# The end of a decoder layer: rows normed and stored before the last expert column, whose tokens' rows are then made per slot and scattered

## The chip, the core and the metric

One core of a Trainium2 chip runs one program that holds a whole decoder layer. The core has TensorE (PE in the profile, its weight loads PEld), VectorE (DVE), ScalarE (ACT), GpSimd (POOL) and SyncE (SP), which here issues nearly all DMAs. The metric is the device time of one execution in microseconds (us). Three runs of the kernel before took 1240.55, 1242.22 and 1242.86 us, so the median is 1242.22 us.

## The reference, cut to what matters

The layer takes 512 tokens of 1024 features through a token mixer, a cross-attention and a mixture of 64 experts, each followed by a residual sum and a layer norm. The change touches the end alone: the last experts, their sum into the rows, and the third norm.

```python
def hierarchical_moe(x, ...):      # each token picks one group, then two experts in it
    ...
    hb = jax.nn.silu(xb @ w_gate[e]) * (xb @ w_up[e])     # D_EXPERT = 256
    return hb @ w_down[e]
    ...
    y_rows = y_rows * row_w[:, None]
    y = jax.ops.segment_sum(y_rows, row_tok, num_segments=N)   # added into the tokens' rows

h = layer_norm(ALPHA * h + ff, ln3_g, ln3_b)    # (r - mean) * rsqrt(var + eps) * g + b, per row of 1024
```

## The kernel before, in words

All expert weights, 192 MB in 64 experts of three matrices of 1 MB, are streamed from HBM once. The experts are served in 21 columns of 128 slots: a column holds one expert with 128 slots, two with 64 or four with 32 (`COLS`). A slot holds one token's row, or none. For each column PE multiplies the gathered rows with the gate and the up matrices (`hidden`, L1190: for a column of four, 64 matmuls each), ACT and DVE make silu(gate) times up (L1195, L1196), PE turns it, DVE copies the turned tile (`hT`), and PE multiplies with the down matrices. `split` (L255 on ACT, L256 on DVE) scales the result by the slot's routing weight and splits it into a high part `yh` and a low part `yl`, which fp32r matmuls can take. `combine` (L1415) then multiplies two columns' `yh` and `yl` with one-hot matrices (slot to token) and DVE adds the eight 128x512 results to `acc` (L1416), the residual rows of all 512 tokens as four tiles `t` of 128 rows, in two halves `nh`. `acc` is named `h` in the trace.

The weights go through ten slots of 1 MB. SP issues a weight's DMA once PE has finished with the slot's former content, so the order of the DMAs is fixed and SP waits in it. The down matrices of the last column come in three pieces of columns (`LASTD`: 512, 256, 256; L184). Every DMA of SP stands in one queue, in the order in which the program issues it.

The last column, number 20, holds four experts with 32 slots each. In the kernel before it ends like this. After the gate matmuls, PE copies halves of `acc` into PSUM by a matmul with the identity (L1484), for tiles 0 to 2; later the column's own one-hot matmuls (L1525) add its part there. Tile 3 is added by DVE (L1535). So no row of any token is complete before the last down matrices are used. Only then come the statistics of all four tiles (L1529, L1531), the inverse root on POOL (L97), and the norm of 512 rows of 1024: on ACT, DVE and POOL for five half tiles (L1574, L1578, L1579), on DVE alone for three (L1585, L1586). Each half tile is stored by its own DMA of 256 KB (L1590). The gain `g3` and the bias `b3` are loaded to all 128 partitions by two DMAs of 512 KB, behind the last weights in SP's queue (L1505, L1506). A loop over overflow slots follows (L1613); in these runs it has no turn.

The order on PE and POOL, and on SP, is made by a scheduler; a `manual_schedule` block keeps DVE (and ACT, where named) in program order.

Of the kernel before, what the change touches and what calls it, by code (L numbers as in the profile page):

```python
# [61 lines left out]
def tile_layer(ctx, tc, x, mem, positions, w_in, attn_sinks, conv_w, conv_b, b_igate, b_fgate, ml_norm_g,  # L62
# [20 lines left out]
    def row(ap1d):  # L83
        return ap1d.rearrange("(o n) -> o n", o=1)
# [14 lines left out]
    class LayerNorm:  # L99
# [7 lines left out]
        def stats(self, c):  # L107
            V.bn_stats(self.st[:, c, :], self.r[:, c * 512:(c + 1) * 512])
# [1363 lines left out]
    zs = {}  # L1472

    def half(nh):
        return slice(nh * 512, (nh + 1) * 512)

    def rows_in(halves):
        if not psl:
            pb.close()
            psl.append(ctx.enter_context(tc.tile_pool(name="psL", bufs=6, space=PSUM, reuse_waits="tile")))  # L1480
        psL = psl[0]
        for nh, t in halves:
            zs[t, nh] = psL.tile([P, 512], F32, name=f"pc_l{t}{nh}", tag="psL")
            T.matmul(zs[t, nh], lhsT=ident, rhs=acc[:, t, half(nh)], start=True, stop=False)  # L1484

    psl = []
# [14 lines left out]
    out_tiles()
    yh = strm.tile([P, 1056], F32R, name="yh_l", tag="wh", bufs=2)[:, :D]
    yl = strm.tile([P, 1056], F32R, name="yl_l", tag="wl", bufs=2)[:, :D]
    g3, b3 = [strm.tile([P, 1056], F32, name=n_, tag="wr", bufs=4)[:, :D] for n_ in ("g3", "b3")]
    nc.sync.dma_start(g3, row(ln3_g).to_broadcast([P, D]))  # L1505
    nc.sync.dma_start(b3, row(ln3_b).to_broadcast([P, D]))  # L1506
    oh = strm.tile([P, 1056], F32R, name="oh_l", tag="wr", bufs=4)[:, :S]
    V.tensor_scalar(oh, iota_f, tokf[:, c:c + 1], None, op0=ALU.is_equal)
    ph = psH.tile([P, 512], F32, name="ph_l", tag="psH")[:, :2 * P].rearrange("p (k n) -> p k n", k=2)
    for k in range(2):  # L1510
        T.transpose(ph[:, k, :], hb[:, k, :], ident)
    hT = hTs[c % 2]
    V.tensor_copy(hT, ph)
    ctx.enter_context(tc.manual_schedule(engines={mybir.EngineType.DVE}))

    def down_part(pd, o, n):
        for k in range(2):
            for sl, w in parts_of(c):
                T.matmul(pd[sl, :], lhsT=hT[:, k, sl], rhs=w['d'][:, k, o:o + n], start=(k == 0), stop=(k == 1))
        split(yh[:, o:o + n], yl[:, o:o + n], pd, wtab[:, c:c + 1])  # L1520

    def combine_part(z, o, n, ts, first, last):
        for y in (yh, yl):
            for t in ts:
                T.matmul(z[t][:, o % 512:o % 512 + n], lhsT=oh[:, t * P:(t + 1) * P], rhs=y[:, o:o + n],  # L1525
                         start=first and y is yh, stop=last and y is yl)
# [6 lines left out]
    def add_last(nh, z):  # L1533
        zs[3, nh] = outt[3][:, half(nh)]
        V.tensor_tensor(zs[3, nh], acc[:, 3, half(nh)], z, ALU.add)  # L1535
# [10 lines left out]
    rows_in([(1, 0), (1, 1), (1, 2)])  # L1546
    (o0, n0), (o1, n1), (o2, n2) = LASTD
    z0, z1 = [{t: zs[t, nh] for t in range(3)} for nh in range(2)]
    pd0 = psH.tile([P, 512], F32, name="pd_l0", tag="psH")
    down_part(pd0, o0, n0)  # L1550
    pd1 = psU.tile([P, 512], F32, name="pd_l1", tag="psU")
    down_part(pd1[:, :n1], o1, n1)
    combine_part(z0, o0, n0, range(3), False, True)
    z0[3] = psH.tile([P, 512], F32, name="pc_l30", tag="psH")
    combine_part(z0, o0, n0, [3], True, True)
    for t in range(3):
        stats(t, 0)
# [12 lines left out]
    stats(2, 1)  # L1570
    shift2(0)

    def norm3(t, nh):
        A.activation(outt[t][:, half(nh)], zs[t, nh], AF.Identity, bias=nb3[:, t:t + 1], scale=rs3[:, t:t + 1])  # L1574

# [3 lines left out]
        G.tensor_tensor(o, o, b3[:, half(nh)], ALU.add)  # L1579
        store(t, nh)  # L1580

    def all3(t, nh):

        o = outt[t][:, half(nh)]
        V.scalar_tensor_tensor(o, zs[t, nh], mv3[:, t, 0:1], g3[:, half(nh)], op0=ALU.subtract, op1=ALU.mult)  # L1585
        V.scalar_tensor_tensor(o, o, rs3[:, t:t + 1], b3[:, half(nh)], op0=ALU.mult, op1=ALU.add)  # L1586
        store(t, nh)

    def store(t, nh):
        nc.sync.dma_start(out[t * P:(t + 1) * P, half(nh)], outt[t][:, half(nh)])  # L1590

    for t, nh in ((0, 0), (0, 1), (1, 0)):
        norm3(t, nh)

    stats(3, 1)
    rsqrt2(2)
    gain3(0, 0)
    shift2(2)
    norm3(2, 0)
    norm3(3, 0)  # L1600
    gain3(0, 1)
    gain3(1, 0)
    all3(1, 1)
    gain3(2, 0)
    gain3(3, 0)
    all3(2, 1)
    all3(3, 1)


    psL = (psl[0], "psL")  # L1610
# [77 lines left out]
```

## Time and profile before

| | |
|---|---|
| median of three runs | 1242.22 us |
| the profiled execution's own time | 1243.13 us |
| its span, first to last instruction | 1241.3 us |
| PE busy | 1145.4 us, 92% |
| DVE busy | 614.3 us, 49% |
| ACT busy | 368.9 us, 30% |
| POOL busy | 123.7 us, 10% |
| mean granted TensorE clock | 0.972 of full speed |

The shares are means over the whole layer and say little about its end. The page's chain of waits is empty for this kernel, so the end is read from the timeline, where each row gives the start, the duration, the engine, the line and tile, and in brackets how long the engine was idle and what released it.

### The profile page before, as it was taken

The numbers are of one execution on the slowest core, as the hardware profiler recorded it, in microseconds if no ns is written. First come the engines' busy times: TensorE is split into PE (matmuls) and PEld (weight loads), VectorE is DVE, ScalarE is ACT, GpSimd is POOL, SyncE is SP. The second block draws the span as 40 slices with busy tenths as digits, with TensorE's granted clock in tenths as the row PEclk, the third lists the DMA queues.
The fourth block names the chain that finished last, engine by engine and source line by source line (L and its number), as shares of the span: only waits on it lengthen the run. The fifth ranks groups of instructions, "written<-read, shape, count | busy, mean of one in ns | idle before, by whom it ended". The sixth has DMA issues, their size and how long they took to land.

```text
span 1241.3 us, 18439 instructions
## 1 busy us (share of the span) xinstructions
PE 1145.4 (92%) x7201; PEld 841.6 (68%) x7201; DVE 614.3 (49%) x1407; ACT 368.9 (30%) x705; POOL 123.7 (10%) x118
## 2 busy tenths in 40 slices
PE   7999999999999999999999989899979998988982
PEld 6777777777787888788888876565735564654641
DVE  5668986533325434584354677834314342431326
ACT  4334355444425423254434341111101011111101
POOL 1330010000010101142101120000000000000003
PEclk8999999999999999999999989999989899998997
DMA  7221112222223233735306059999999999999993
GB/s 189 84 70 51 52 51 68 60 77 68 69 84 85 85 100 99 237 102 169 103 18 234 5 237 374 400 418 419 411 419 417 406 407 418 395 419 419 418 404 128
DMA packets 119658, 269.09 MB, mean 217 GB/s; under 512 B 18704, under 2 KB 79120, under 8 KB 95504
## 3 DMA queue, kind: packets, MB, share of 16 engines
q1 hardware_dynamic: 119280, 266.83, 57.4%
q8 instruction: 58, 0.95, 0.3%
q10 hardware_dynamic: 288, 1.05, 0.3%
q14 instruction: 32, 0.26, 0.1%
HBM read 265.76 MB, written 2.10 MB: 216 GB/s over the span
## 4 chain that ended last, share of the span: by engine, by line


## 5 line engine op out<-in xcount | busy, mean ns | idle before, releaser
L239 ACT CAST wh<-wr 128x1024 fp32r<-128x1024 f32 (+1 forms) x106 | 111.1, 1050 | 257.3 <-issue 82.0
L240 DVE TENSOR_TENSOR wl<-wr,wh 128x1024 fp32r<-128x1024 f32 (+1 forms) x80 | 99.5, 1245 | 152.1 <-ACT wh L239 149.1
L1190 PE MATMUL pu<-wu,arenaL 128*32 128x256 f32 (+2 forms) x1024 | 103.1, 441 | 30.4 <-DMA wu<-in_w_up_dram 30.3
L240 POOL TENSOR_TENSOR wl<-wr,wh 128x1024 fp32r<-128x1024 f32 x26 | 64.7, 2489 | 443.6 <-ACT wh L239 406.7
L1190 PEld LDWEIGHTS pu<-wu,arenaL 128*32 128x32 f32 (+2 forms) x1024 | 53.9, 134 | 75.3 <-DMA wu<-in_w_up_dram 41.2
L1196 DVE TENSOR_TENSOR arenaR<-arenaR,pu 128x256 f32<-128x256 f32 x21 | 13.1, 622 | 175.5 <-ACT arenaR L1195 175.5
L1190 PE MATMUL pu<-wg,arenaL 128*32 128x256 f32 (+2 forms) x1024 | 83.7, 390 | 6.4 <-DMA wg<-in_w_gate_dram 6.4
L1247 PE MATMUL px<-G,h2h 128*128 128x256 f32 (+1 forms) x320 | 81.1, 292 | 0.0
L1271 PE MATMUL pd<-wd,arenaR 128*32 128x512 f32 (+2 forms) x480 | 77.2, 596 | 3.0 <-DMA wd<-in_w_down_dram 2.8
L1190 PEld LDWEIGHTS pu<-wg,arenaL 128*32 128x32 f32 (+2 forms) x1024 | 46.7, 121 | 46.7 <-issue 10.5
L1248 PE MATMUL px<-G,h2l 128*128 128x256 f32 (+1 forms) x320 | 77.6, 282 | 0.0
L1195 ACT ACTIVATE arenaR<-pu 128x256 f32<-128x256 f32 x21 | 8.1, 386 | 211.2 <-PE pu L1190 211.2
L1247 PEld LDWEIGHTS px<-G,h2h 128*128 128x128 f32 x320 | 60.9, 190 | 7.3 <-issue 7.3
L255 ACT ACTIVATE yh<-pd,wtab 128x512 fp32r<-128x512 f32 x40 | 27.2, 687 | 124.9 <-PE pd L1271 110.7
L1415 PE MATMUL pc<-yh,oh 128*128 128x512 f32 x144 | 59.7, 415 | 1.9 <-DVE h L1416 1.8
L1248 PEld LDWEIGHTS px<-G,h2l 128*128 128x128 f32 x320 | 61.1, 191 | 0.1
L1416 DVE TENSOR_TENSOR h<-h,pc 128x512 f32<-128x512 f32 x72 | 49.3, 686 | 17.5 <-PE pc L1415 16.6
L1415 PE MATMUL pc<-yl,oh 128*128 128x512 f32 x144 | 56.8, 395 | 0.0
L1271 PEld LDWEIGHTS pd<-wd,arenaR 128*32 128x32 f32 (+2 forms) x480 | 22.4, 118 | 44.6 <-issue 35.5
L97 POOL TENSOR_TENSOR rs<-ve,pow_h 128x2 f32<-128x2 f32 x2 | 1.9, 956 | 496.5 <-DVE ve L1539 496.5
L1170 ACT ACTIVATE arenaL<-px,gbk 128x256 f32<-128x256 f32 (+1 forms) x44 | 24.2, 555 | 79.1 <-PE px L1248 70.1
L256 DVE SCALAR_TENSOR_TENSOR yl<-pd,wtab,yh 128x512 fp32r<-128x512 f32 x40 | 29.7, 749 | 32.3 <-ACT yh L255 32.0
(451 smaller groups left out, 2655.5 us busy)
## 6 DMA issues: line engine op xcount, KB each, us to landing
wg<-in_w_gate_dram SPq DMA_DIRECT2D x64, 1024.0 KB, 12.5
wu<-in_w_up_dram SPq DMA_DIRECT2D x64, 1024.0 KB, 14.6
wd<-in_w_down_dram SPq DMA_DIRECT2D x60, 1024.0 KB, 13.2
wr<-in_w_in_dram SPq DMA_DIRECT2D x50, 512.0 KB, 3.6
wr<-in_w_xkv_dram SPq DMA_DIRECT2D x16, 512.0 KB, 4.0
wr<-in_w_att_branch_dram SPq DMA_DIRECT2D x8, 512.0 KB, 4.0
wr<-in_w_ml_branch_dram SPq DMA_DIRECT2D x8, 512.0 KB, 4.0
wr<-in_w_mix_out_dram SPq DMA_DIRECT2D x8, 512.0 KB, 3.9
```

Source lines behind the costliest of these rows:

```text
L239: A.copy(hi, raw)
L240: (G if i % 4 == 3 else V).tensor_tensor(lo, raw, hi.bitcast(F32), ALU.subtract)
L255: A.activation(hi, src, AF.Copy, scale=scale)
L256: V.scalar_tensor_tensor(lo, src, scale, hi.bitcast(F32), op0=ALU.mult, op1=ALU.subtract)
L1170: A.activation(XT[:, k, :n], px[:, j, :n], AF.Identity, scale=gbk[:, 0, k:k + 1], bias=gbk[:, 1, k:k + 1])
L1190: T.matmul(pu[sl, u * 256:(u + 1) * 256], lhsT=XT[:, k, o + sl.start:o + sl.stop], rhs=w[what][:, k, :], start=(k == 0), stop=(k == NK - 1))
L1196: V.tensor_tensor(hb.rearrange("s k p -> s p k"), hs.rearrange("s (p k) -> s p k", k=2), pu[:, 256:512].rearrange("s (p k) -> s p k", k=2) ...
L1247: T.matmul(px[:, j, :n], lhsT=h2hv[:, t, 2 * c + j, :], rhs=g[:, t, :n], start=(t == 0), stop=False)
L1248: T.matmul(px[:, j, :n], lhsT=h2lv[:, t, 2 * c + j, :], rhs=g[:, t, :n], start=False, stop=(t == NT - 1))
L1271: T.matmul(pd[sl, :], lhsT=hT[:, k, sl], rhs=w['d'][:, k, nh * 512:(nh + 1) * 512], start=(k == 0), stop=(k == 1))
L1415: T.matmul(pc, lhsT=oh[:, t * P:(t + 1) * P], rhs=y[:, ns], start=(i == 0), stop=(i == len(mms) - 1))
L1416: V.tensor_tensor(acc[:, t, ns], acc[:, t, ns], pc, ALU.add)
```

## The change

Before the last column's matmuls, the change treats `acc` as if the last column did not exist: all 512 rows get their statistics, norm, gain and bias (`rows_meanwhile`, hooked in behind the gate matmuls) and are stored by four DMAs of 512 KB. DVE's part of the statistics is placed by hand between the adds of `combine`. Tokens that have a slot in the last column are stored with a wrong row by this. Their right rows are made a second time, one row per slot: `gsel` picks the row of each slot's token out of `acc` by fp32 matmuls (`slot_rows`, into `zf`), and `same`, a 128x128 matrix that says which slots have the same token, adds `yh` and `yl`. One tile of 128 rows is then normed on DVE into `fin`, and an indirect DMA of POOL scatters its rows to `out` by the tokens' numbers `tok_u`; empty slots have number 4096 and are left out. The scatter waits for all four stores, since it writes over some of their rows.

The gain and bias rows come as two DMAs of 2x512 in ACT's queue, long before, and are spread to 128 partitions by four matmuls with K=4 (`spread_row`) and four copies on ACT. The identity matmuls into PSUM, the 12 pairs of one-hot matmuls of the last column (L1525) and the two 512 KB loads go. The one-hot `oh` stays for the overflow loop, but is made last. The read of the loop's count (`nov_r`, one TENSOR_LOAD on each engine) moves ahead of the last column.

```diff
     c = NMAIN - 1
...
+    rows4 = work.tile([4, 512], name="rows4", at=0)
+    for i, v in enumerate((ln3_g, ln3_b)):
+        nc.scalar.dma_start(rows4[2 * i:2 * i + 2, :], v.rearrange("(a n) -> a n", a=2))
...
+    V.tensor_scalar(diag, ident, tokl, None, op0=ALU.mult)
+    T.matmul(prow, lhsT=ones, rhs=diag, start=True, stop=True)
+    V.tensor_scalar(same, prow, tokl, None, op0=ALU.is_equal)
+    for t in range(NT):
+        V.tensor_scalar(gsel[:, t, :], prow, -BIGIDX, rowid[:, t:t + 1], op0=ALU.add, op1=ALU.is_equal)
...
     run(combine(before, "last"))
-    hooks = {(0, 7): lambda: rows_in([(0, 0), (0, 1), (0, 2)])}
-    hb = hidden_of(c, (psU, "psU"), hooks)
+    ctx.enter_context(tc.manual_schedule(engines={mybir.EngineType.DVE, mybir.EngineType.Activation}))
     nov_r = nc.values_load(ovi[0:1, 32:33], min_val=0, max_val=NOV)
...
+    def spread_row(i):
+        pg = psL.tile([P, 512], F32, name=f"pg{i}", tag="psL")
+        T.matmul(pg, lhsT=ident[:4, i:i + 1].to_broadcast([4, P]), rhs=rows4, start=True, stop=True)
+        A.copy((g3, b3)[i // 2][:, half(i % 2)], pg)
+    def slot_rows(i):
+        o, w_ = LASTD[i]
+        zf.append(psL.tile([P, 512], F32, name=f"zf{i}", tag="psL")[:, :w_])
+        for t in range(NT):
+            T.matmul(zf[i], lhsT=gsel[:, t, :], rhs=acc[:, t, o:o + w_], start=(t == 0), stop=False)
+    def rows_meanwhile():
...
+        wstream.ahead(used[0] + COLS[c][0] + len(wslots))
+        out_tiles()
+        for i in (0, 1):
+            spread_row(i)
+        for t in range(2):
+            for nh in range(2):
+                stats(t, nh)
+        rsqrt2(0)
...
+        gain_row(0)
+        shift2(2)
+        norm_row(2)
+        norm_row(3)
+        bias_row(0, G)
+        gain_row(1)
+        bias_row(1, G)
+        gain_row(2)
+        slot_rows(0)
+    hb = hidden_of(c, (psU, "psU"), {(0, 7): rows_meanwhile})
+    slot_rows(1)
     for k in range(2):
         T.transpose(ph[:, k, :], hb[:, k, :], ident)
+    slot_rows(2)
     hT = hTs[c % 2]
+    gain_row(3)
     V.tensor_copy(hT, ph)
+    bias_row(2, V)
+    for i, (o, w_) in enumerate(LASTD):
...
+        split(yh[:, o:o + w_], yl[:, o:o + w_], pd, wtab[:, c:c + 1])
+        if i == 1:
+            bias_row(3, V)
+    for i, (o, w_) in enumerate(LASTD):
         for y in (yh, yl):
+            T.matmul(zf[i], lhsT=same, rhs=y[:, o:o + w_], start=False, stop=(y is yl))
+        for j in range(0, w_, 256):
+            V.bn_stats(stf[:, (o + j) // 256, :], zf[i][:, j:j + 256])
+    V.bn_aggr(mvf, stf)
+    V.tensor_scalar(vef, mvf[:, 1:2], LN_EPS / ALPHA ** 2, None, op0=ALU.add)
+    rsqrt_cols(rsf, vef, 1)
+    for z, (o, w_) in zip(zf, LASTD):
+        V.scalar_tensor_tensor(fin[:, o:o + w_], z, mvf[:, 0:1], g3[:, o:o + w_], op0=ALU.subtract, op1=ALU.mult)
+    for nh in range(2):
+        V.scalar_tensor_tensor(fin[:, half(nh)], fin[:, half(nh)], rsf, b3[:, half(nh)], op0=ALU.mult, op1=ALU.add)
+    G.indirect_dma_start(out, bass.IndirectOffsetOnAxis(ap=tok_u, axis=0), fin, None, bounds_check=S - 1, oob_is_err=False)
+    V.tensor_scalar(oh, iota_f, tokl, None, op0=ALU.is_equal)
```

Here `stats` is a BN_STATS of one half tile of `acc` (L1504) and, after the second half, a BN_AGGR (L1506); `norm_row`, `gain_row` and `bias_row` each treat 128 rows of 1024 on ACT, DVE, and POOL or DVE; `bias_row` also issues the store.

Two places show the new order. The first is DVE around the last `combine`, from the `yl` parts of column 19 (`yl_10119`) to the adds to `acc` (`h_3991`; `pc_last` are the results of `combine`). Before:

```order
L256 SCALAR_TENSOR_TENSOR yl_10119<-pd_10121,wtab,yh_10118 128x512
L256 SCALAR_TENSOR_TENSOR yl_10119<-pd_10132,wtab,yh_10118 128x512
L1416 TENSOR_TENSOR h_3991<-h_3991,pc_last_10152 128x512
L1416 TENSOR_TENSOR h_3991<-h_3991,pc_last_10158 128x512
L1416 TENSOR_TENSOR h_3991<-h_3991,pc_last_10164 128x512
```

And now (`oh_l` holds `same`, `arenaL` holds `gsel`, `st` and `mv` the statistics):

```order
L256 SCALAR_TENSOR_TENSOR yl_10119<-pd_10121,wtab,yh_10118 128x512
L1490 TENSOR_SCALAR oh_l<-prow,tokf 128x128
L1492 TENSOR_SCALAR arenaL<-prow,arenaR 128x128
L256 SCALAR_TENSOR_TENSOR yl_10119<-pd_10132,wtab,yh_10118 128x512
L1492 TENSOR_SCALAR arenaL<-prow,arenaR 128x128 x3
L1416 TENSOR_TENSOR h_3991<-h_3991,pc_last_10171 128x512
L1416 TENSOR_TENSOR h_3991<-h_3991,pc_last_10177 128x512
L1499 TENSOR_LOAD ovi
L1504 BN_STATS st_10147<-h_3991 128x6
L1416 TENSOR_TENSOR h_3991<-h_3991,pc_last_10183 128x512
L1504 BN_STATS st_10147<-h_3991 128x6
L1416 TENSOR_TENSOR h_3991<-h_3991,pc_last_10189 128x512
```

Five selection matrices now stand ahead of the first add, and a load, four statistics and an aggregation between the first add and the last. PE's last `combine` matmuls wait for these adds, since `pc_last` has two PSUM tiles.

The second place is PE in the last column, from the last gate matmul (`wg`) to the first up matmul (`wu`). Before:

```order
L1190 MATMUL pu_10200<-wg_10060,arenaL 32x256
L1484 MATMUL pc_l_10239<-h_3991,ident 128x512
L1484 MATMUL pc_l_10241<-h_3991,ident 128x512
L1484 MATMUL pc_l_10243<-h_3991,ident 128x512
L1190 MATMUL pu_10200<-wu_10072,arenaL 32x256
```

And now (`pg` are the spread gain and bias, `zf` the slots' rows):

```order
L1190 MATMUL pu_10241<-wg_10060,arenaL 32x256
L1549 MATMUL pg_10292<-arenaR,ident 128x512
L1549 MATMUL pg_10295<-arenaR,ident 128x512
L1549 MATMUL pg_10312<-arenaR,ident 128x512
L1549 MATMUL pg_10315<-arenaR,ident 128x512
L1557 MATMUL zf_10333<-h_3991,arenaL 128x512 x4
L1190 MATMUL pu_10241<-wu_10072,arenaL 32x256
```

Eight fp32 matmuls of 512 columns stand where three stood.

## Rows read from the trace of the kernel before

**Rows 1.** Windows of two stages: us, busy us by engine (instructions), TensorE clock, DMA.

```profile
1194.90:1206.80 11.90, 10.63 (x135) 5.12 (x134) 0.69 (x1) 0.02 (x1) 0.00 (x0) 1.00 1.02 401
1220.50:1236.20 15.70, 0.00 (x0) 0.00 (x0) 14.68 (x25) 3.60 (x5) 9.72 (x7) 0.62 0.27 99
```

**Rows 2.** Timeline, PE in the last column: start, us, line, shapes, [idle before].

```profile
1194.89 3.66 PE L1190 MATMUL pu<-wg,arenaL 128*32 128x256 f32 x64
...
1198.49 2.84 PE L1484 MATMUL pc_l<-h,ident 128*128 128x512 f32 x6
...
1203.11 3.64 PE L1190 MATMUL pu<-wu,arenaL 128*32 128x256 f32 x58 [1.21 <-DMA wu<-in_w_up_dram]
...
1207.86 0.44 PE L1511 MATMUL ph_l<-ident,arenaR 128*128 128x128 f32 x2 [1.11 <-DVE arenaR L1196]
...
1210.80 2.79 PE L1519 MATMUL pd_l<-wd,arenaR 128*32 128x512 f32 x32
...
1217.20 1.07 PE L1519 MATMUL pd_l<-wd,arenaR 128*32 128x256 f32 x16
```

**Rows 3.** Timeline, DVE around the last combine.

```profile
1187.50 0.75 DVE L256 SCALAR_TENSOR_TENSOR yl<-pd,wtab,yh 128x512 fp32r<-128x512 f32 x1 [0.96 <-ACT yh L255]
...
1188.16 1.36 DVE L1416 TENSOR_TENSOR h<-h,pc_last 128x512 f32<-128x512 f32 x2
...
1195.00 0.69 DVE L1416 TENSOR_TENSOR h<-h,pc_last 128x512 f32<-128x512 f32 x1 [0.23 <-PE pc_last L1415]
```

**Rows 4.** Groups by form, 1180 to 1242 us: count, busy us, mean ns, idle before.

```profile
L1416 DVE TENSOR_TENSOR h<-h,pc_last 128x512 f32<-128x512 f32 x8 | 5.5, 687 | 2.0 <-PE pc_last L1415 2.0
...
L1168 DVE TENSOR_SCALAR arenaL<-px,gbk 128x128 f32<-128x128 f32 x1 | 0.4, 411 | 1.5 <-ACT arenaL L1170 1.5
```

**Rows 5.** The line that loads the loop's count: duration in ns (min/median/max), start.

```profile
L1491 PEldq TENSOR_LOAD <-ovi x1: 488/488/488, 1204.9 to 1204.9; - x1
...
L1491 DVEq TENSOR_LOAD <-ovi x1: 812/812/812, 1235.4 to 1235.4; - x1
```

**Rows 6.** Timeline, the last column's split, statistics and last result.

```profile
1212.79 0.69 ACT L255 ACTIVATE yh_l<-pd_l,wtab 128x512 fp32r<-128x512 f32 x1 [5.62 <-PE pd_l L1519]
...
1218.85 0.48 DVE L256 SCALAR_TENSOR_TENSOR yl_l<-pd_l,wtab,yh_l 128x256 fp32r<-128x256 f32 x1
...
1219.26 0.68 DVE L1529 BATCH_NORM_STATS2 st<-out 128x6 f32<-128x512 f32 x1
...
1220.57 0.21 DVE L1531 BATCH_NORM_AGGREGATE mv<-st 128x2 f32<-128x12 f32 x1
...
1224.38 1.21 POOL L97 TENSOR_TENSOR rs<-ve,pow_h 128x2 f32<-128x2 f32 x1 [1.81 <-DVE ve L1539]
...
1235.36 0.75 DVE L1586 SCALAR_TENSOR_TENSOR out<-out,rs,b 128x512 f32<-128x512 f32 x1
```

**Rows 7.** Operations on 128x1024, whole trace: groups by form, and one line (ns).

```profile
L1081 ACT ACTIVATE h<-h,ln_nb,ln_rs 128x1024 f32<-128x1024 f32 x4 | 5.0, 1246 | 2.7 <-DVE ln_nb L119 2.7
...
L240 POOL TENSOR_TENSOR wl<-wr,wh 128x1024 fp32r<-128x1024 f32 x26 | 64.7, 2489 | 443.6 <-ACT wh L239 406.7 <-DVE pT L592 36.9
...
L1097 DVE TENSOR_TENSOR h<-h,bbc x4: 1224/1225/1226, 784.0 to 795.9; 128x1024 f32<-128x1024 f32 x4
```

**Rows 8.** One line of DVE at the end: from PSUM, and from SBUF beside POOL.

```profile
L1585 DVE SCALAR_TENSOR_TENSOR out<-pc_l,mv,g x2: 735/736/736, 1228.0 to 1231.9; 128x512 f32<-128x512 f32 x2
L1585 DVE SCALAR_TENSOR_TENSOR out<-out,mv,g x1: 1743/1743/1743, 1233.6 to 1233.6; 128x512 f32<-128x512 f32 x1
```

**Rows 9.** DMA issues: count, KB each, us from issue to landing.

```profile
out_dram<-out SPq DMA_DIRECT2D x1, 256.0 KB, 2.6
...
gbc<-in_ln_g_dram SPq DMA_DIRECT2D x1, 512.0 KB, 3.4
...
bif<-in_b_igate_dram SPq DMA_DIRECT2D x1, 2.0 KB, 7.1
```

**Rows 10.** A window in which PE waited for weights, columns as in rows 1.

```profile
1124.00:1128.00 4.00, 1.47 (x10) 0.38 (x14) 0.00 (x0) 0.00 (x0) 0.00 (x0) 0.64 1.02 424
```

More of the change, by code (lines that the diff above doesn't have):

```diff
@@ L1471, in tile_layer @@
     ve3, rs3, nb3 = [small.tile([P, NT], F32, name=n) for n in ("ve3", "rs3", "nb3")]
-    zs = {}
+    stf, mvf = small.tile([P, 4, 6], F32, name="stf"), small.tile([P, 2], F32, name="mvf")
+    vef, rsf = [small.tile([P, 1], F32, name=n) for n in ("vef", "rsf")]
+    tok_u = small.tile([P, 1], U32, name="tok_u")
+    xt1 = XTs[1].rearrange("p k n -> p (k n)")
+    gsel = xt1[:, 0:S].rearrange("p (t n) -> p t n", t=NT)
+    diag, fin = xt1[:, S:S + P], xt1[:, 1024:2048]
+    rows4 = work.tile([4, 512], name="rows4", at=0)
@@ new lines, in tile_layer @@
+    for i, v in enumerate((ln3_g, ln3_b)):
+        nc.scalar.dma_start(rows4[2 * i:2 * i + 2, :], v.rearrange("(a n) -> a n", a=2))
+    oh = strm.tile([P, 1056], F32R, name="oh_l", tag="wr", bufs=4)
+    oh, same = oh[:, :S], oh[:, S:S + P]
+    g3, b3 = [strm.tile([P, 1056], F32, name=n_, tag="wr", bufs=4)[:, :D] for n_ in ("g3", "b3")]
+    tokl = tokf[:, c:c + 1]
+    V.tensor_copy(tok_u, tokl)
+    V.tensor_scalar(diag, ident, tokl, None, op0=ALU.mult)
+    prow = psX.tile([P, 512], F32, name="prow", tag="psX")[:, :P]
@@ L1474, in half @@
+    T.matmul(prow, lhsT=ones, rhs=diag, start=True, stop=True)
+    V.tensor_scalar(same, prow, tokl, None, op0=ALU.is_equal)
+    for t in range(NT):
+        V.tensor_scalar(gsel[:, t, :], prow, -BIGIDX, rowid[:, t:t + 1], op0=ALU.add, op1=ALU.is_equal)
     def half(nh):
         return slice(nh * 512, (nh + 1) * 512)
[L1477 to L1484, printed above, removed]
@@ L1501, in tile_layer @@
[L1501 to L1508, printed above, removed]
@@ L1509, in tile_layer @@
[L1509 to L1526, printed above, removed]
+    zs = {}
     def stats(t, nh):
@@ L1580, in gain3 @@
         store(t, nh)
[L1582 to L1587, printed above, removed]
     def store(t, nh):
         nc.sync.dma_start(out[t * P:(t + 1) * P, half(nh)], outt[t][:, half(nh)])
[L1592 to L1610, printed above, removed]
+    def out_tiles():
+        for i in range(2):
+            pool, tag = wslots[wstream.next % wstream.total]
+            wstream.next += 1
+            t = pool.tile([P, 2048], F32, name=f"out{i}", tag=tag)
+            outt.extend([t[:, 0:D], t[:, D:2 * D]])
+    def norm_row(t):
+        A.activation(outt[t], acc[:, t, :], AF.Identity, bias=nb3[:, t:t + 1], scale=rs3[:, t:t + 1])
@@ new lines, in gain_row, with bias_row @@
+    def gain_row(t):
+        V.tensor_tensor(outt[t], outt[t], g3, ALU.mult)
+    def bias_row(t, on):
+        on.tensor_tensor(outt[t], outt[t], b3, ALU.add)
+        nc.sync.dma_start(out[t * P:(t + 1) * P, :], outt[t])
+    def spread_row(i):
[7 more added lines that the diff above has]
+            T.matmul(zf[i], lhsT=gsel[:, t, :], rhs=acc[:, t, o:o + w_], start=(t == 0), stop=False)
@@ new lines, in tile_layer @@
+    pb.close()
+    psL = ctx.enter_context(tc.tile_pool(name="psL", bufs=6, space=PSUM, reuse_waits="tile"))
+    zf = []
+    def rows_meanwhile():
+        for t in range(NT):
+            for nh in range(2):
+                zs[t, nh] = acc[:, t, half(nh)]
+        wstream.ahead(used[0] + COLS[c][0] + len(wslots))
[6 more added lines that the diff above has]
+        rsqrt2(0)
+        for nh in range(2):
+            stats(2, nh)
+        shift2(0)
+        norm_row(0)
+        norm_row(1)
+        for i in (2, 3):
+            spread_row(i)
+        for nh in range(2):
+            stats(3, nh)
+        rsqrt2(2)
+        gain_row(0)
[7 more added lines that the diff above has]
+        slot_rows(0)
@@ new lines, in tile_layer @@
+    hb = hidden_of(c, (psU, "psU"), {(0, 7): rows_meanwhile})
+    yh = strm.tile([P, 1056], F32R, name="yh_l", tag="wh", bufs=2)[:, :D]
+    yl = strm.tile([P, 1056], F32R, name="yl_l", tag="wl", bufs=2)[:, :D]
+    slot_rows(1)
+    ph = psH.tile([P, 512], F32, name="ph_l", tag="psH")[:, :2 * P].rearrange("p (k n) -> p k n", k=2)
+    for k in range(2):
+        T.transpose(ph[:, k, :], hb[:, k, :], ident)
+    slot_rows(2)
+    hT = hTs[c % 2]
+    gain_row(3)
+    V.tensor_copy(hT, ph)
+    bias_row(2, V)
@@ new lines, in tile_layer @@
+    pds = []
+    for i, (o, w_) in enumerate(LASTD):
+        pd = psL.tile([P, 512], F32, name=f"pd_l{i}", tag="psL")[:, :w_]
+        for k in range(2):
+            for sl, w in parts_of(c):
+                T.matmul(pd[sl, :], lhsT=hT[:, k, sl], rhs=w['d'][:, k, o:o + w_], start=(k == 0), stop=(k == 1))
+        split(yh[:, o:o + w_], yl[:, o:o + w_], pd, wtab[:, c:c + 1])
+        if i == 1:
+            bias_row(3, V)
+    for i, (o, w_) in enumerate(LASTD):
+        for y in (yh, yl):
+            T.matmul(zf[i], lhsT=same, rhs=y[:, o:o + w_], start=False, stop=(y is yl))
+        for j in range(0, w_, 256):
+            V.bn_stats(stf[:, (o + j) // 256, :], zf[i][:, j:j + 256])
@@ new lines, in tile_layer @@
+    V.bn_aggr(mvf, stf)
[3 more added lines that the diff above has]
+        V.scalar_tensor_tensor(fin[:, o:o + w_], z, mvf[:, 0:1], g3[:, o:o + w_], op0=ALU.subtract, op1=ALU.mult)
+    for nh in range(2):
+        V.scalar_tensor_tensor(fin[:, half(nh)], fin[:, half(nh)], rsf, b3[:, half(nh)], op0=ALU.mult, op1=ALU.add)
+    G.indirect_dma_start(out, bass.IndirectOffsetOnAxis(ap=tok_u, axis=0), fin, None, bounds_check=S - 1, oob_is_err=False)
@@ L1611, in tile_layer @@
+    V.tensor_scalar(oh, iota_f, tokl, None, op0=ALU.is_equal)
+    psL = (psL, "psL")
     off = keep.tile([P, 1], F32, name="off")
```

37 lines of the change are left out of this document (removed).

## The prediction

> **What bounds the kernel now.** I first read the windows of the last two stages, since the page's shares are means over the whole layer. While the last weights come, the DMA engines are busy all the time (share 1.02, 401 GB/s); after 1220.5 us PE does nothing, DVE is busy 14.68 of 15.70 us and the DMA engines 0.27 of the time [rows 1]. So the layer streams weights, and then norms 512 rows with hardly anything beside it. That stretch is what the change goes for.
>
> Then the timeline of PE. The gate matmuls of the last column start at 1194.89 and are done when the identity matmuls start, at 1198.49. The up matmuls wait 1.21 us for weights and end at 1203.11 + 3.64 = 1206.75. The turn starts 1.11 later, the first down matmul at 1210.80 [rows 2]. On DVE the last result is there at 1235.36 + 0.75 = 1236.11 [rows 6]; the last store lands 2.6 us later [rows 9], at 1238.7, and the span ends at 1241.3, another 2.6 later. I keep these last 2.6 us. The profiled execution took 1243.13 us, 0.9 above the median of 1242.22: I work with shifts inside its span and take the net shift from the median.
>
> **The change part by part.** I follow the path from the last combine on, before against now.
>
> *Ahead of the adds.* DVE now makes five 128x128 selections. The nearest row is 0.41 us for a 128x128 operation that reads PSUM [rows 4]. Two stand ahead of the second `yl`, where DVE had idled 0.96 us [rows 3]; I take them as covered. Three stand behind it and count whole: 3 x 0.41 = 1.2. The bounds are 0 and 5 x 0.41 = 2.05. The first add moves from 1188.16 [rows 3] to 1189.4.
>
> *Between the adds.* From the first add's start to the last one's, DVE took 1195.00 - 1188.16 = 6.84 us [rows 3], of which it idled up to 2.0, waiting for PE [rows 4]. Now seven adds of 0.69, one load of 0.81 [rows 5], four statistics of 0.68 and an aggregation of 0.21 [rows 6] stand there: 4.83 + 0.81 + 2.72 + 0.21 = 8.57. DVE, not PE, sets the pace, and PE's last matmuls wait for its adds through two PSUM tiles. That is 1.7 more; the bounds are 0 (all of it hidden) and 3.7 (the 2.0 idle stays). The last add starts at 1189.4 + 8.6 = 1198.0, 3.0 later.
>
> *Gate.* PE started the gate matmuls 0.1 ahead of the last add. I keep that and add PE's own load, 0.49 [rows 5]: start 1198.4, end 1202.0, which is 3.5 later. The SP queue waits here too, since the last down weights go into slots that the gate matmuls free; but these weights are now used only at 1217 (below), 6.6 later than before, and the stores stand behind them in the same queue, so they cannot push them back.
>
> *Eight fp32 matmuls ahead of the up matmuls.* Three identity matmuls of that size took 2.84 us, 0.95 each [rows 2]; the spread with K=4 has no row, and I price it as the same (its bounds are 0 and this). 8 x 0.95 = 7.6, to 1209.6. The up weights were there at 1203.11, so the wait of 1.21 goes and PE's own work is late in its place. The up matmuls take what the gate ones took, 3.66, to 1213.2: 6.5 later than before.
>
> *To the down matmuls.* `slot_rows(1)`, four matmuls of half the width, 1.9, covers the 1.11 of silu and product. Then the turn, 0.44, and `slot_rows(2)`, 1.9: the first down matmul starts at 1217.5, not 1210.80. The three down parts take 2.79 + 1.07 [rows 2], to 1221.3, with the second done at 1220.3.
>
> *What DVE, ACT and POOL do for all rows meanwhile.* ACT copies gain and bias (four of 0.69, as [rows 6]) and norms four tiles of 1.25 [rows 7], done by about 1211. DVE's gains take 1.22 each and POOL's two bias tiles 2.49 each [rows 7]. Beside POOL, a DVE operation on two SBUF operands took 1.74, against 0.74 with one operand in PSUM [rows 8], so I let these wait for each other in full: POOL's first bias 1208.5 to 1211.0, then the third gain, POOL's second bias 1212.2 to 1214.7, the fourth gain to 1215.9, and the copy of `hT` by 1216.4. PE is not ready for it before 1217.5, so this cover holds with 1.1 us to spare; without it the last result would move one for one. The Trainium skill (SBUF — State Buffer, "SBUF: two separate sides") calls this shared port pair an exclusive lock, which those rows agree with. It adds that GpSimd cannot write the descriptors of its own DMA while DVE runs an operation in a 2-port mode. A one-hot of 128x512 stands on DVE right behind the last result here; by that rule the scatter would wait for it, between 0.48 and 0.75 us (the two widths in rows 6), and the sum below would be up to 1236.9.
>
> *Tail.* The second `yl`: 1220.3 + 0.48 (ACT, taken as DVE's 0.48 for that width) + 0.48 = 1221.3. Then `bias_row(3)`, 1.22, stands ahead of the third `yl`: 1222.5 + 0.48 = 1223.0. The matmuls with `same` run along. Four statistics of half width, 0.34 each: 1224.4. Aggregation and epsilon, 0.21 each: 1224.8. Three operations from PSUM, 0.74 + 2 x 0.48 = 1.7, cover POOL's root (1.21 [rows 6]): 1226.5. Two of 0.75 [rows 6]: **1228.0**. Before it was 1236.1, so 8.1 us are gained here: 15.7 us of norms go and some 5 remain, but they start later.
>
> *The scatter.* No row shows a DMA that POOL issues. 512 KB on a quiet queue landed in 3.4 us [rows 9]; I add one POOL operation, 1.21 [rows 6], for making its list: 4.6. The bounds are 2.6 (the last store) and 7.1 + 1.2 = 8.3 (the slowest small DMA [rows 9]). The value is near the lower end, since that row is the one of its size. 4.6 instead of 2.6 costs 2.0. The last row store is issued at 1222.5 and, at 3.4, lands at 1225.9, 2.1 ahead of the scatter that waits for it.
>
> The Trainium skill (DMA: Bandwidth & Descriptors, "Anatomy of one DMA — SWDGE (gpsimd) path") fits a DMA of GpSimd with 2.0 us plus its bytes over 436 GB/s, which is an estimate of 3.2 us here. By it the sum would be 1.4 lower, 1234.7. No run here shows it yet.
>
> *Sum.* -8.1 + 2.0 = -6.1: span 1235.2, own time 1237.0, and from the median 1242.2 - 6.1 = **1236.1 us**. Its own range, with the bounds of the single terms rarely all on one side, is 1232.5 to 1239.5.
>
> **Rivals.**
>
> *More is hidden.* The selections and statistics cost PE nothing: 3.0 less, and with the scatter at 2.6 another 2.0: 1231.1. For it: DVE idled 2.0 us in that stretch. Against: 8.57 us of work in 6.84.
>
> *The gain shrinks.* The scatter is at its upper bound (+3.7), or the last store lands late: at 7.1 it lands at 1229.6 and holds the scatter up by 1.6. Or PE's clock falls in the stretched combine: in a window in which PE was busy 1.47 of 4.00 us the granted clock was 0.64 of 2.4 GHz [rows 10], and with the gate's 3.6 us at 1.2 GHz 3.6 are lost. Against the clock: PE would still be busy some 8 of 11 us there. One of these gives 1238 to 1240, two 1241.5.
>
> *Slower: the scatter does not spread over the DMA engines.* All 16 moved 401 to 424 GB/s [rows 1, 10], one of them about 26; 512 KB through one take 20 us instead of 4.6: 1236.1 + 15.4 = 1251.5. It decides from 4.6 + 6.1 = 10.7 us on. For it: no row shows a list of rows from POOL; against: every 128-row DMA here landed in microseconds.
>
> *It does not do what it says.* The first store is ready at 1211.0, behind the last weights in SP's queue, so most of the storing lies beside the last column's matmuls and not beside the weights. That costs nothing while the fourth store lands before 1228.0, so the time is the forecast's.
>
> **How the numbers follow.** Forecast 0.60 (with the last rival, which has its time), more hidden 0.10, shrunk gain 0.17, slow scatter 0.13. About 0.2%, 2.5 us, is what a measurement of this kernel can tell: faster is below 1239.7. Faster 0.60 + 0.10 + 0.05 of the shrunk case = 0.75; same the other 0.12; slower 0.13. The range from 1231.0 to 1241.5 leaves out the slow scatter and a little at the low end.
>
> **What would show it.** In the profile after: DVE without idle time between the adds and the gate matmuls some 3.5 us later; the up matmuls with no wait for weights, starting near 1209.6; `hT` copied before PE asks for it; the last DVE result near 1228; POOL's DMA landing within 5 us of it. I am wrong in the size if the gate starts as early as before; wrong in the sign if the scatter takes over 10.7 us.

## The result, and the profile after

Five runs of the changed kernel took 1231.22 to 1235.53 us, with a median of **1233.27**; five of the kernel before, beside them, a median of 1242.22. The ratio is 0.9924, with a 95% interval of 0.991 to 0.9938: faster by 9 us. The forecast was 1236.1, in a range of 1231.0 to 1241.5.

The profiled executions differ by 11.8 us of span (1241.3 and 1229.5), but 2.2 of these arose before the change begins: the first `yl` of column 19 starts at 1185.78 before and 1183.62 after, and in later profiles of kernels with the same code up to there anywhere from 1183.97 to 1188.27. So I count every time from this start (**"+"** below), before:

```profile
1185.78 0.75 DVE L256 SCALAR_TENSOR_TENSOR yl<-pd,wtab,yh 128x512 fp32r<-128x512 f32 x1 [4.87 <-ACT yh L255]
```

From it to the end of the span it took 55.52 us before, and 45.88 after: 9.64 less, where the prediction had 6.1.

First the windows of the two stages that answer to [rows 1] (us, busy by engine, granted clock, DMA):

```profile
1194.05:1206.60 12.55, 12.55 (x83) 5.42 (x82) 8.38 (x16) 6.67 (x8) 4.45 (x4) 0.86 1.03 392
1217.60:1224.10 6.50, 1.50 (x10) 0.97 (x6) 6.43 (x15) 0.48 (x1) 0.56 (x1) 0.83 0.22 84
```

While the weights come, DVE, ACT and POOL are now busy 8.4, 6.7 and 4.5 us where they had 0.7 together. The stretch of DVE alone at the end is 6.5 us, not 15.7. But the clock in the first window is 0.86, where it had been 1.00 [rows 1].

DVE around the last combine, as [rows 3]:

```profile
1183.62 0.75 DVE L256 SCALAR_TENSOR_TENSOR yl<-pd,wtab,yh 128x512 fp32r<-128x512 f32 x1 [4.14 <-ACT yh L255]
...
1185.30 0.34 DVE L1492 TENSOR_SCALAR arenaL<-prow,arenaR 128x128 f32<-128x128 f32 x1
1185.56 0.74 DVE L256 SCALAR_TENSOR_TENSOR yl<-pd,wtab,yh 128x512 fp32r<-128x512 f32 x1
1186.22 0.86 DVE L1492 TENSOR_SCALAR arenaL<-prow,arenaR 128x128 f32<-128x128 f32 x3
1186.99 1.28 DVE L1416 TENSOR_TENSOR h<-h,pc_last 128x512 f32<-128x512 f32 x2
1188.18 0.69 DVE L1504 BATCH_NORM_STATS2 st<-h 128x6 f32<-128x512 f32 x1
...
1193.39 1.45 DVE L1416 TENSOR_TENSOR h<-h,pc_last 128x512 f32<-128x512 f32 x2
```

The first add starts at +3.37 (before +2.38), the last ends at 1194.84, and no row between them shows DVE waiting. The load of the loop's count, as [rows 5], runs beside the adds:

```profile
L1499 DVEq TENSOR_LOAD <-ovi x1: 543/543/543, 1186.9 to 1186.9; - x1
```

PE in the last column, as [rows 2]:

```profile
1194.05 3.66 PE L1190 MATMUL pu<-wg,arenaL 128*32 128x256 f32 x64
1197.64 3.69 PE L1549 MATMUL pg<-arenaR,ident 4*128 4x512 f32 x8
1201.27 5.40 PE L1557 MATMUL zf<-h,arenaL 128*128 128x512 f32 x8
1206.59 3.66 PE L1190 MATMUL pu<-wu,arenaL 128*32 128x256 f32 x64
...
1214.06 3.65 PE L1612 MATMUL pd_l<-wd,arenaR 128*32 128x512 f32 x48
```

No bracket: PE waits for nothing here, not for weights either. The spread and `zf0` are four matmuls each, in eight passes of the same width; the spread takes 3.69 us and `zf0` 5.40. In windows of 1 us the granted clock is 1.00 up to 1201.05, so through nearly all of the spread, and 0.50 from 1202.05 to 1204.05.

DVE beside it, and at the end:

```profile
1202.62 1.22 DVE L1540 TENSOR_TENSOR out<-out,g 128x1024 f32<-128x1024 f32 x1
1204.64 2.50 DVE L1540 TENSOR_TENSOR out<-out,g 128x1024 f32<-128x1024 f32 x1 [0.80 <-ACT out L1537]
...
1212.43 0.42 DVE L1605 COPY arenaR<-ph_l 128x256 f32<-128x256 f32 x1
...
1222.62 1.41 DVE L1627 SCALAR_TENSOR_TENSOR arenaL<-arenaL,rsf,b 128x512 f32<-128x512 f32 x2
```

POOL over the same time:

```profile
1203.55 5.84 POOL L1543 TENSOR_TENSOR out<-out,b 128x1024 f32<-128x1024 f32 x2 [4.50 <-ACT b L1550]
...
1224.33 1.21 POOL L1628 DMA_INDIRECT out_dram<-arenaL,tok_u  x1 [2.44 <-POOLq L1635]
```

And the scatter's queue (packets, MB, share) and its time from issue to landing:

```profile
q0 software_dynamic: 144, 0.02, 0.0%
...
out_dram<-arenaL,tok_u POOLq DMA_INDIRECT x1, 3.1
```

One gain takes 1.22 us alone and 2.50 beside POOL's bias. The last DVE result is there at 1224.03, and the span ends 5.47 us later (before: 5.2). The scatter's queue moved 0.02 MB, where 128 rows of 4 KB are 0.52; 140 of its 144 packets are under 512 bytes, so four carry a row.

### The profile page after: what moved, and what is told of

Read it like the earlier page. It is cut to its first block, busy times and chain, and to the rows that moved or that the text cites. A ratio compares the mean times of both kernels' runs of the same rounds, so it can differ in the third digit from the quotient of the medians.

```text
span 1229.5 us, 18450 instructions
## 1 busy us (share of the span) xinstructions
PE 1148.0 (93%) x7205; PEld 844.4 (69%) x7205; DVE 615.7 (50%) x1418; ACT 372.0 (30%) x708; POOL 123.0 (10%) x117
## 5 line engine op out<-in xcount | busy, mean ns | idle before, releaser
L240 DVE TENSOR_TENSOR wl<-wr,wh 128x1024 fp32r<-128x1024 f32 (+1 forms) x80 | 99.3, 1242 | 151.6 <-ACT wh L239 150.8
L1196 DVE TENSOR_TENSOR arenaR<-arenaR,pu 128x256 f32<-128x256 f32 x21 | 13.1, 621 | 160.5 <-ACT arenaR L1195 160.5
```

The lines of the kernel that those rows point to most:

```text
L240: (G if i % 4 == 3 else V).tensor_tensor(lo, raw, hi.bitcast(F32), ALU.subtract)
L1196: V.tensor_tensor(hb.rearrange("s k p -> s p k"), hs.rearrange("s (p k) -> s p k", k=2), pu[:, 256:512].rearrange("s (p k) -> s p k", k=2) ...
```

## The experiments

All kernels are edits of the changed one. Their marks, from starts in the timelines; "product" is the hidden product (L1196), whose turn the down matmuls wait for:

| | gate starts | up ends | product | down starts | span ends |
|---|---|---|---|---|---|
| before | +9.11 | +20.97 | +21.42 | +25.02 | +55.52 |
| changed | +10.43 | +26.63 | +27.20 | +30.44 | +45.88 |
| spread over 128 rows | +10.44 | +24.75 | +25.32 | +28.56 | +44.11 |
| without `zf0` | +10.44 | +24.64 | +25.22 | +28.44 | +44.02 |
| without row norms | +10.45 | +26.65 | +27.16 | +30.45 | +45.23 |
| rows late | +10.45 | +24.96 | +25.47 | +28.76 | +54.22 |
| adds first | +10.12 | +26.27 | +26.85 | +30.08 | +45.42 |
| early preparation | +9.44 | +21.21 | +22.66 | +25.41 | +41.09 |
| both | +9.10 | +20.95 | +25.23 | +27.97 | +43.43 |
| early, biases on DVE | +9.47 | +20.35 | +20.92 | +24.16 | +39.52 |

**The change's main part undone: rows late.**

```diff
-  norm_row(0..3), gain_row(0..3), bias_row(0..3)   # in the last column
   ... bn_stats(stf, zf) ...
+  norm_row(0..3), gain_row(0..3), bias_row(0..3)   # here
   V.bn_aggr(mvf, stf)
```

> One part of the change undone: norm, gain, bias and store of the four row tiles wait until the last column's slots have their statistics, instead of running while its weights come. Nothing is left out. Theory A (the gain is that these rows lie under the wait for weights): from the last yl of the column before to the end it takes 53 to 58 us instead of 45.9: four gains and four biases of 1.2 to 2.9 us on VectorE and GpSimd, a last 512 KB store of some 4 us, and the scatter behind it; the whole gain over the kernel before (its stretch is 55.5 us) is lost. Theory B (the gain lies elsewhere: fewer accumulations at the end, another start of the weights): no more than 3 us of it are lost.

1240.85 us in one execution; the kernel before, beside it, had a median of 1242.66. The end is at +54.22. Theory A: 8.3 of the 9.6 us are lost, so most of the gain is that these rows lie beside the last weights and PE's work. On DVE the three gains that run first now stand behind the last statistics, where nothing hides them:

```profile
1219.60 5.63 DVE L1540 TENSOR_TENSOR out<-out,g 128x1024 f32<-128x1024 f32 x3
```

**The rows left out.** `norm_row` and `gain_row` do nothing, `bias_row` stores `acc`.

> The norm, gain and bias of the four row tiles in the last column are left out (their statistics stay, and the four 512 KB stores take the accumulated rows instead), so the output is not the reference's. ScalarE loses 4 passes of 1.25 us, VectorE 4 gains and 2 biases, GpSimd 2 biases of 2.5 to 2.9 us. Theory A (all of it lies under TensorE's work, as predicted at no cost): the stretch from the last yl of the column before to the end changes by less than 1 us; what can go is the 1.22 us bias that stands between two splits at the end. Theory B (the rows' work holds VectorE or ScalarE, and with it the hidden product and the copies that TensorE waits for): 2 us or more are gained.

The up matmuls end at +26.65, as with the rows, and the end comes 0.65 earlier. Theory A: norm, gain and bias cost 0.65 us (the statistics are still in).

**The scatter with all rows, and a plain store.**

```diff
-    V.tensor_copy(tok_u, tokl)
+    V.tensor_copy(tok_u, iota_p)                # slot p to row p
```

> The last column's rows are scattered to rows 0 to 127 of the output, all slots, instead of to the tokens of the few filled slots, so the output is not the reference's. In the changed kernel the scatter moved 0.02 MB in 144 packets, 140 of them under 512 bytes, and landed 3.1 us after its issue: the last column held few tokens, and the rows of empty slots were dropped. The prediction priced it as 512 KB at 4.6 us, bounds 2.6 to 8.3. Theory A (the price holds for full slots): the scatter lands 4.0 to 5.5 us after issue with 0.5 MB in its queue, and the end comes 1 to 2.5 us later after the last result. Theory B (one row, one descriptor, on few engines): 8 us or more to landing, the end 5 us or more later. Theory C (rows make no difference): 3.1 us again.

```diff
-    G.indirect_dma_start(out, ...tok_u..., fin, ...)
+    nc.sync.dma_start(out[0:P, :], fin)
```

> The scatter replaced by one plain 512 KB store of the same tile to rows 0 to 127 (the output is not the reference's). The prediction took a scatter at 4.6 us against a store at 2.6, 2.0 us for it. The changed kernel's scatter, with few rows in it, is 1.2 us of GpSimd and 3.1 us to landing; with all 128 rows the end came 1.35 us later. Theory A (a store of 512 KB has as much to move as the full scatter and no cheaper start): its end lies within 1 us of the changed kernel's, 5 to 6 us behind the last product. Theory B (the scatter's start on GpSimd is dear, as the prediction took it): the end comes 1.5 to 2.5 us earlier than the full scatter's, so at least 0.5 us earlier than the changed kernel's.

The queue and the landing of the full scatter (the share is of a window of 17 us), then the landing of the store:

```profile
q0 software_dynamic: 144, 0.52, 8.3%
...
out_dram<-arenaL,tok_u POOLq DMA_INDIRECT x1, 4.5
```

```profile
out_dram<-arenaL SPq DMA_DIRECT2D x1, 512.0 KB, 4.1
```

From the last result to the end of the span it takes 6.82 us with all rows (1224.38 to 1231.2), 6.40 with the store (1226.90 to 1233.3) and 5.47 in the changed kernel. Theory A for the scatter: the price of 4.6 us was right for full slots (4.5). The store's end (+46.77) lies 0.9 us behind the changed kernel's, as theory A had it, but 6.40 behind the last result is over its 5 to 6; theory B is out, since a full scatter ends only 0.4 us later than a store of the same size. What the prediction had wrong is what is in the slots: the last column holds four tokens, by the packets above, and the rows of empty slots are dropped. The page of the Trainium skill weighed in the prediction (DMA: Bandwidth & Descriptors, "Anatomy of one DMA — SWDGE (gpsimd) path") gives an estimate of 3.2 us for 512 KB; the full scatter took 4.5, and the measurement decides.

**`zf0` left out** (and `start=True` at its first later matmul).

> The four groups of matmuls that put the last column's tokens' accumulated rows into the first half of the slot rows (zf0, 5.40 us of TensorE between the gate and the up matmuls) are left out, so the output is not the reference's. Theory A (in the last column TensorE's queue alone sets the end): the up matmuls end 5.4 us earlier and the end of the kernel comes 5 to 5.4 us earlier after the last yl of the column before. Theory B (VectorE takes over): its product of the hidden units stands in its queue behind the third gain product, which runs 2.50 us beside GpSimd's bias additions and ends at 1207.1, so the product starts only 3 to 4 us earlier than now, and the end gains 2.5 to 4 us. Theory C (the weights' transfers take over): an up or a down matmul waits for a weight transfer, and the gain ends there.

All three theories missed. 5.40 us of PE went, and the end came 1.86 earlier; no engine or transfer made PE wait. Its own matmuls became slower:

```profile
1199.11 4.77 PE L1549 MATMUL pg<-arenaR,ident 4*128 4x512 f32 x8
1203.81 5.91 PE L1190 MATMUL pu<-wu,arenaL 128*32 128x256 f32 x64
```

A window there, columns as in the first fence, shows PE busy all the time with the clock at 0.50, its 1.2 GHz level:

```profile
1202.00:1208.00 6.00, 6.00 (x43) 2.28 (x45) 4.33 (x4) 5.20 (x6) 2.99 (x2) 0.50 1.07 372
```

The fall comes with the end of the spread and hits whatever stands behind it.

**The spread over 128 rows.**

```diff
-    rows4 = work.tile([4, 512], ...)
+    rows4 = work.tile([P, 512], ...); G.memset(rows4, 0.0)
-    T.matmul(pg, lhsT=ident[:4, i:i + 1].to_broadcast([4, P]), rhs=rows4, ...)
+    T.matmul(pg, lhsT=ident[:, i:i + 1].to_broadcast([P, P]), rhs=rows4, ...)
```

> The four matmuls that spread the last norm's gain and bias over the partitions contract over 128 rows (rows 4 to 127 set to zero) instead of 4; nothing else changes. In the changed kernel they start 3.6 us after the gate matmuls, and the granted clock falls behind their start to 0.80 and 0.77 of full speed, so that the next stage, 16 plain fp32 matmuls (zf0), takes 5.40 us where eight of the same shape take 3.7. Theory A (the four-row contraction lets the clock fall): with 128 rows the clock stays near 1.00 there, zf0 takes 3.6 to 3.9 us, and the stretch from the last column's first gate matmul to its last up matmul shrinks by 1.5 to 1.9 us, the end by as much. Theory B (the clock falls for another reason, the stalls of the combine before it or a turn that comes anyway): zf0 stays at 5.0 to 5.6 us and nothing else moves. One look cannot see 1.7 us in the total; it is read from the stretch.

Its `zf0`, and a window over it:

```profile
1202.96 3.60 PE L1558 MATMUL zf<-h,arenaL 128*128 128x512 f32 x8
```

```profile
1202.00:1206.00 4.00, 4.00 (x11) 1.71 (x9) 2.43 (x3) 4.00 (x6) 0.67 (x1) 1.00 1.05 385
```

In the changed kernel the same window reads:

```profile
1202.00:1206.00 4.00, 4.00 (x7) 1.61 (x6) 3.20 (x4) 3.74 (x5) 2.45 (x1) 0.65 1.05 376
```

`zf0` (four matmuls in eight passes, not the 16 of the text above) takes 3.60 instead of 5.40, and the end comes 1.77 earlier: theory A. Timed:

> The spread of the last norm's gain and bias over 128 rows instead of 4 once more, timed. The one look showed the stretch from the last column's first gate matmul to its last up matmul 1.9 us shorter. Theory A (the clock's fall was on the path to the end): the median lies 1.5 to 2 us under the changed kernel's 1233.3, near 1231.5, as far as runs that differ by 4 us among themselves can tell. Theory B (hidden behind VectorE): no difference.

1230.94 us (1230.28 to 1234.04), ratio to before 0.9908 (0.9894 to 0.9922): the size is as expected, but the interval overlaps the changed kernel's, so the traces carry this, not the timing. The profile of the timed kernel ends at +44.03, as the first did.

"Rows late" spoke against it: there the spread still has four rows, and `zf0` took 3.70 us. So it ran again.

> The kernel with the rows' norms undone to the end once more, for the granted clock alone: its spread still contracts over 4 rows, yet in its first profile the clock stayed at 1.00 there, zf0 took 3.70 us, and the stretch from the first gate matmul to the end of the up matmuls was 14.5 us, as with 128 rows. Theory A (the four-row matmuls let the clock fall in some executions and not in others): a second execution may show 5.1 to 5.4 us for zf0 and 16.2 us for the stretch; if it does, it is settled that one kernel can go both ways. Theory B (what runs beside them decides, here that ScalarE, VectorE and GpSimd have no row work): 3.70 us and 14.5 us again; one such repeat speaks for B without settling it. The rest: 54 us from the last yl of the column before to the end again, less or more by the clock alone.

1243.21 us, with the end at +55.94. `zf0` in the first execution, and in the second:

```profile
1202.55 3.70 PE L1557 MATMUL zf<-h,arenaL 128*128 128x512 f32 x8
```

```profile
1203.22 5.40 PE L1557 MATMUL zf<-h,arenaL 128*128 128x512 f32 x8
```

So one kernel goes both ways. Of the eight profiles with the four-row spread in the last column, seven show the fall there; of the five changed kernels' profiles without it, none (two spread over 128 rows in the same place, three have no spread in that column). What decides in the eighth stays open, and so does why four rows let the clock fall. The other falls of the clock in the changed kernel's trace, from 600 us to the last column, stand behind waits of PE, as in [rows 10]; this one does not.

**The preparation early.** (One line of the edit is shown.) The spread (over 128 rows) goes between gate and up of column 17, the selections into column 19, the one-hot for overflow ahead of the hidden product.

```diff
+        mid = {17: {(0, 7): spread_early}, 19: {(0, 7): select_early}}.get(c, {})
-        hb = hidden_of(c, (psU, "psU"), {})
+        hb = hidden_of(c, (psU, "psU"), mid)
```

> The preparation of the last column is moved ahead of it, into waits for weights: the spread of gain and bias (contracting over 128 rows) between the gate and up matmuls of the column three places before, the selections of the last column's tokens between those of the column before; and the one-hot for overflow columns no longer stands behind the scatter. What remains in the last column is as in the changed kernel. Theory A (TensorE's queue sets the end): the first add comes 1.0 us earlier after the last yl of the column before, the up matmuls start 3.7 us sooner for the spread and 1.8 us for the clock, so the up matmuls end some 6.5 us earlier and the end comes 5.5 to 6.5 us earlier. Theory B (VectorE and GpSimd take over): the gains of the four row tiles, 2.50 us each beside a bias on GpSimd, stand before the hidden product in VectorE's queue and let it start at best some 4 us earlier; the end gains 3 to 4.5 us. Theory C (the weights take over): an up or a down matmul waits on a transfer, and less than 3 us are gained.

1230.24 us (1227.67 to 1231.68), ratio 0.9899 (0.9882 to 0.9915). From the start of `yl` the gain is 4.79 us, between theories A and B. The up matmuls end 5.42 earlier, the product only 4.54, and two rows of DVE say why:

```profile
1204.54 3.10 DVE L1565 TENSOR_TENSOR out<-out,g 128x1024 f32<-128x1024 f32 x1 [0.22 <-ACT out L1562]
1208.25 1.90 DVE L1617 TENSOR_SCALAR ohl<-iota_f,tokf 128x512 fp32r<-128x512 f32 x1 [0.61 <-PE pu L1190]
1210.07 0.60 DVE L1196 TENSOR_TENSOR arenaR<-arenaR,pu 128x256 f32<-128x256 f32 x1
```

The gain and the one-hot, which takes 0.48 in the changed kernel, run beside POOL's biases, ahead of the product. Theory C has its part too: the up matmuls waited 0.28 us for weights, PE's weight loads 0.6 us for the last down weights, and the down matmuls took 4.65 us instead of 3.65. Of the 4.79, 1.8 is the clock, which the spread over 128 rows gives by itself.

The mark leaves out what the moved work might cost ahead of it. PE waits there for the down weights of column 19, 1.45 us here and 1.43 in the changed kernel, so no cost shows; the median fell by 3.0.

**Adds first, and both.** (The engines' names are shortened.)

```diff
+    ctx.enter_context(tc.manual_schedule(engines={DVE, Activation}))
     run(combine(before, "last"))
-    ctx.enter_context(tc.manual_schedule(engines={DVE, Activation}))
```

> The order of VectorE is fixed from before the last combine on, so that its eight additions stand ahead of the row statistics, which in the changed kernel run between them. Theory A (the statistics between the additions hold the combine back): the gate matmuls start 0.8 to 1.5 us earlier after the last yl of the column before, and the end comes as much earlier. Theory B (the additions wait for TensorE's results as it is, and the statistics only fill gaps): gate start and end move by less than 0.3 us, and the row norms start up to 3 us later.

1232.38 us, ratio 0.9923 (0.9906 to 0.994). The gate starts 0.31 earlier and the end comes 0.46 earlier: just over B's bound, far under A's.

> Early preparation and additions ahead of statistics together. Theory A (TensorE's queue alone): the gains add, 6.5 to 8 us less than the changed kernel at the end. Theory B (VectorE's queue with gains, statistics and hidden product binds once the preparation is out of the way): no more than the early preparation alone within 0.5 us, since the same work stands before the hidden product in VectorE's queue whichever way round.

1230.48 us, ratio 0.9907 (0.989 to 0.9925). A is wrong, and B too: the end is 2.34 us later than with the early preparation alone. With the statistics behind all adds the second pair of norms starts later, the gains run into POOL's work, and PE waits:

```profile
1207.49 3.29 DVE L1565 TENSOR_TENSOR out<-out,g 128x1024 f32<-128x1024 f32 x1 [0.22 <-ACT out L1562]
...
1211.74 0.44 PE L1627 MATMUL ph_l<-ident,arenaR 128*128 128x128 f32 x2 [3.00 <-DVE arenaR L1196]
```

What cost the changed kernel nothing, DVE's queue, costs 3 us of PE's time in this profile, once PE is ready sooner. The medians, 0.24 us apart, do not settle the 2.34.

**Early preparation, all biases on DVE.**

```diff
-        bias_row(0, G); gain_row(1); bias_row(1, G); gain_row(2)
+        gain_row(1); bias_row(0, V); gain_row(2); bias_row(1, V)
```

> The early preparation again, with the biases of the first two row tiles on VectorE (1.22 us each) instead of GpSimd (where VectorE's gains beside them take 2.5 to 3.1 us), and the overflow one-hot again behind the scatter. Theory A (VectorE's queue, slowed beside GpSimd, held the hidden product back): the product starts 0.6 us after the up matmuls end instead of 1.5 us, the end comes 0.7 to 1.5 us earlier than with the early preparation alone, 39.6 to 40.4 us after the last yl of the column before. Theory B (the last down weights bind: their transfers were waited for at the end of the down matmuls): the product starts earlier, the down matmuls wait longer, and the end gains less than 0.4 us.

**1227.56 us** (1226.98 to 1229.77), ratio 0.9878 (0.9857 to 0.9899), an interval wholly under the changed kernel's: it beats that and the kernel before; with the early preparation's interval it overlaps. The mark moves as theory A says, 1.57 us: every operation on DVE now takes its 1.22 us, and the product follows the up matmuls by 0.57 instead of 1.45.

```profile
1206.41 1.22 DVE L1568 TENSOR_TENSOR out<-out,b 128x1024 f32<-128x1024 f32 x1
1208.20 0.61 DVE L1196 TENSOR_TENSOR arenaR<-arenaR,pu 128x256 f32<-128x256 f32 x1 [0.58 <-ACT arenaR L1195]
```

But only 0.88 of the 1.74 us by which the product comes earlier is DVE's queue. The rest is that the up matmuls took 3.66 us from first start to last end, without the wait for weights that made them 4.55; the down matmuls took 3.83 instead of 4.65. That may be owed to this one execution, for in column 19, ahead of the mark, PE ran slowly:

```profile
1182.94 5.32 PE L1274 MATMUL pd<-wd,arenaR 128*32 128x512 f32 x26 [1.45 <-DMA wd<-in_w_down_dram]
```

In the early preparation's profile these matmuls take 3.62, behind the same wait. The clock was 0.61 on average from 1182.94 to 1187.28, which put the mark off by 1.7 us, while the transfers went on at 421 GB/s. So theory B is not ruled out by the marks; for A speaks that the median fell by 2.7. The biases and the one-hot were moved together, and their shares are not told apart.

## Why the prediction was right, and where its terms were off

The mechanism is the one predicted: the row norms moved under the wait for weights, PE's own work became late in place of that wait, and the rest comes per slot at the end. "Rows late" gives back 8.3 of the 9.6 us, and 10.1, the whole gain, in the execution in which the clock fell as it did in the changed kernel; "without row norms" shows that nothing of norm, gain and bias but 0.65 us is on the path. It is the sizes that were off, 3.5 us too pessimistic in the stretch, 2.8 in the median. Part of the closeness is luck: with the spread over 128 rows, so without the fall of the clock, the stretch shrinks by 11.4 us where 6.1 were predicted, and that kernel's median, 1230.94, lies just under the range. A slowdown that the prediction did not foresee there hid part of its pessimism.

- *Selections*: +1.2 predicted, +1.0 measured. Two of them delayed the second `yl` by 0.2 us after all, but each took 0.34 us where 0.41 was taken.
- *Between the adds*: +1.7 predicted, +0.3 measured. From the first add to the end of the last: 7.85 us (7.53 before), where 8.57 and 0.69 for the last add were summed. The load, priced at 0.81, took 0.54 beside the adds, and operations that last 0.69 each start 0.6 us apart (two adds in 1.28). The gate starts 1.32 later, not 3.5, since PE's load, priced at 0.49, cost nothing either. This is the largest miss.
- *Eight fp32 matmuls*: 7.6 predicted, 8.95 measured (1197.64 to 1206.59), the one term that was too small. The four-row spread was priced like the others and takes just that; what it does to the clock of the next stage was not seen. The clock was in the rivals, but for PE's idle time in the combine; there PE waited 0.87 us once, and the clock stayed at 1.00.
- *Up matmuls*: their end +6.5 predicted, +5.66 measured, the last two misses together. The wait for weights is gone, as said.
- *`hT`*: copied by 1212.85, 1.2 ahead of the first down matmul; 1.1 was predicted. The third gain took twice its time beside POOL, as [rows 8] had it; the fourth ran alone.
- *Tail*: from the first down matmul to the last result 10.0 us, 10.5 predicted. The last result came 9.9 us earlier, not 8.1.
- *Scatter*: +2.0 predicted, +0.3 measured. The price of a full one was right; that all 128 slots are filled was assumed and is false. This is 1.7 of the 3.5 us.

Of the rivals, "more is hidden" (1231.1) came half true: less delay and a cheap scatter, but the clock took back 1.8. The slow scatter did not happen even with all rows. That most of the storing lies beside the last column's matmuls came true: the four stores were issued from 1207.15 on, behind the last weights, and the fourth by 1219.41, 4.6 us ahead of the last result. That the one-hot behind the last result holds the scatter up, by the rule of the Trainium skill (SBUF — State Buffer, "SBUF: two separate sides") on descriptors, did not show: from the last result to the end it is 5.47 us with it there and 5.42 without (early preparation). That DVE and POOL get in each other's way shows elsewhere, in gains of 2.50 and 3.10 us beside POOL.

## What to carry to other kernels

Move work under a wait and then list what stands in the next stage's queue in its place: here it was PE's preparation, which belonged into earlier waits, and then DVE's gains beside POOL. Before pricing an indirect DMA, ask how many of its rows are real. Sum one engine's operations by the distance of their starts, not by their durations. A mark near the end is sharper than the whole time, but it moves too when something slows ahead of it.

## What was not expected of the hardware

- The granted clock fell to 0.50 at the end of matmuls that contract over 4 rows, with PE busy without a gap, in 7 of 8 profiles; with 128 rows, for the same eight passes of 3.7 us, it stayed at 1.00 in both. It cost 1.8 us of `zf0`, and 1.1 + 2.25 us of the spread and the up matmuls where `zf0` was left out.
- A scatter in which nearly all rows are out of bounds still makes 144 packets; it landed in 3.1 us, a full one in 4.5.
- The same code up to column 19 reached its `yl` between 1183.62 and 1188.27 us in different executions. Differences of 2 us in the end are to be read from a mark near it.
